# Convolution taps, level sums and gate copies moved between engines in a four-part transformer kernel on one Trainium2 core

## The chip, the cores and the metric

The kernel runs on one core of a Trainium2 chip. The metric is the device time of one execution in microseconds (us). A core has five engines with queues of their own: TensorE (PE; its weight loads are listed apart as PEld), VectorE (DVE), ScalarE (ACT), GpSimd (POOL) and SyncE (SP), which here issues the loads of weights. Each engine takes its instructions in the order of the program and waits on semaphores for the others. PSUM, where TensorE writes, is used as eight banks.

## The reference, cut to what matters

There are 256 tokens of width 1024. They pass an even layer (a convolution branch and gated linear attention), a PEER layer (128 chosen experts of 16384 a token), an odd layer (attention with forget gates), a second PEER layer, and then a block of sliding-window attention with spatial gating (mix2) and an MLP with a three-tap convolution. The parts that the change touches:

```python
def conformer_conv(val, gate, conv_w, conv_b, ln_g, ln_b):      # even layer, 512 channels, 31 taps
    u = val * jax.nn.sigmoid(gate)
    y = lax.conv_general_dilated(u, w, window_strides=(1,), padding=[(CONV_WIDTH - 1, 0)], ...)
    y = y + conv_b.astype(y.dtype)
    return jax.nn.silu(layer_norm(y, ln_g, ln_b))
...
def step(state, inp):                                           # even layer, gated linear attention
    b = jnp.cumsum(gi, axis=2)
    o_inter = jnp.einsum('bhtk,bhkv->bhtv', qi * jnp.exp(b), state)
    decay = jnp.exp(jnp.where(causal[:, :, None], diff, -jnp.inf))
    attn = jnp.einsum('bhtk,bhsk,bhtsk->bhts', qi, ki, decay)
    o = o_inter + jnp.einsum('bhts,bhsv->bhtv', attn, vi)
...
def block(args):                                                # PEER
    ht, et, gt = args
    act = jax.nn.gelu(jnp.einsum('td,ted->te', ht, u[et]), approximate=False)
    return jnp.einsum('te,ted->td', gt * act, v[et])
...
q = rms_norm(q.reshape(B, S, FOX_HEADS, FOX_HD), q_g)           # odd layer
k = rms_norm(k.reshape(B, S, FOX_HEADS, FOX_HD), k_g)
...
x = x + conv_gated_mlp(rmsnorm(x, ffn_norm[l]), w_up[l], conv_w[l], conv_b[l], w_down[l])
```

## The kernel before

Activations lie with the width on the 128 partitions and the tokens along them. Every dense product takes its float32 operands in two parts, a rounded one (`_hi`) and the rest (`_lo`), so that one block of weights costs three products: hi x hi, lo x hi, hi x lo. Weights pass a **Stream**: SyncE loads a block of 512 KB into `w_raw`, ScalarE rounds it to `w_hi` (L337), VectorE subtracts for `w_lo` (L353). All dense products are issued at line L452.

What runs beside a projection is written as generators. `tick` (L900) steps the list **flow** once and gives **bg**, the background, an allowance of ns; so the place of small steps between the large products follows from their yields. `banks(pj, pa, pl, po)` gives the PSUM banks that projections and auxiliary products go round in.

The even layer (0 to about 175 us) projects v (`va`, four steps, `natural`), the channels of the convolution (`aval`, `agate`), k and q (`kq`) and r. `gated` makes a channel block `ub` = val x sigmoid(gate) (the tanh of `sg` on ScalarE, L941, and the product L942). Of its 31 taps 23 go to VectorE as multiply-adds `yc` in the background (`conv`, L769), and the first 8 (`CONV_PE`) to TensorE: GpSimd scales eight diagonals `dg` (`taps`, L656), `conv_pe` multiplies them with ub into a bank `pe`, ScalarE copies it to `yp` (L783). `decays` makes the decays of the attention. `inner`, once for each of 8 pairs of head and token half, makes seven levels of scores `pm`, VectorE masks them to `sm` (L822, L823), and seven products add them up in `oT`, after which products with the state follow. A chain of `inner` begins in each tick. `head_norm` (products `o_ps`, `ob`) and `layer_norm` (`mu_b`, `var_ps`, `rs_b`) give the rows `yf` of the output projection, whose blocks (`rows`) are added as their rows become ready.

A PEER layer runs 64 gate cycles (369 to 604 us, and 1351 to 1586 us), each of 4 tokens: ScalarE makes one-hot rows `oa` (L1168, four; L1174), VectorE their partners `ob`, TensorE the gates `g` of the cycle into PSUM and 24 products `pu`, the experts' activations; ScalarE and VectorE write gelu(pu) into X (L1271 on ScalarE, L1274 and L1275 for the later part). `put` (below) takes the gates of the cycle out of PSUM: where X has activations already, they are multiplied (L1190), elsewhere copied (L1192, VectorE). The copied part shrinks from 308 to about 56 columns in the 64 cycles.

```python
                    for lo, hi, x in spans(c, NCH):
                        nc.vector.tensor_copy(x[:, :, t0:t0 + GT], gt[:, lo:hi])
```

In the odd layer `qk_out` squares each q or k block (`qk_sq`, L1527) and after each second k block adds `quad` to flow, which begins `rms_heads`: eight small products `qn_ps`, the root, and their spread `qn_rb`. `c_ps` are the sums of the forget gates; `pt` are transposes of the attention. `mix2` uses banks 4 to 7 for projections and 0 to 3 for the rest. In the MLP `normed` makes the normalised input of the later products: GpSimd multiplies by `rb` (L1749) and by the gain (L1750), ScalarE rounds (L1752), GpSimd subtracts to `hn_lo` (L1754), for 8 blocks.

Of the kernel before, what the change touches and what calls it, by code (L numbers as in the profile page):

```python
# [20 lines left out]
P = 128  # L21
# [20 lines left out]
EV_ROWS = (4, 5, 6, 7, 0, 1, 2, 3)  # L42
CONV_PE = 8
U_SLACK = 1300
# [334 lines left out]
def body(ctx: ExitStack, tc: tile.TileContext, a, out, phases=(0, 6)):  # L379
# [6 lines left out]
    class Banks:  # L386
# [5 lines left out]
        def set(self, banks):  # L392
            self.banks, self.i = banks, 0
# [244 lines left out]
    def even():  # L638
        banks((0, 1), (2, 3))
        with even_pool as es:  # L640
# [7 lines left out]
            tri64, = masks(sp, 3, 4)  # L648
            dgs = deque()

            def taps():
                c = len(dgs) + pe_done
                if c < 4:
                    dg = tp.tile([P, CONV_PE, P], F32, name="dg", tag="dg")
                    for j in range(CONV_PE):
                        nc.gpsimd.tensor_scalar(dg[:, j], ident, col("convw", c * CONVW + j), None, op0=OP.mult)  # L656
                    dgs.append(dg)

            f2 = lambda t: t.rearrange("p a b -> p (a b)")
# [5 lines left out]
            def parts(k0, n):  # L665
                for k in range(k0, k0 + n):
                    if k in split_k:
                        i = split_k.index(k)
                        split_to(y[0][:, i], y[1][:, i], yf[:, k])
                    ready.add(k)  # L670

# [17 lines left out]
            def decays():  # L689
# [7 lines left out]
                proj_small(h, gws, ps[:16, :S], 16)  # L697
                while norm["steps"] is not None:
                    yield
# [64 lines left out]
            def conv(c):  # L764
                nc.vector.tensor_scalar(yc[:, c], ub[:, c, CONV_PE:CONV_PE + S], col("convw", c * CONVW + CONV_PE),
                                        col("convb", c), op0=OP.mult, op1=OP.add)
                yield 300
                for j in range(CONV_PE + 1, CONVW):
                    nc.vector.scalar_tensor_tensor(yc[:, c], ub[:, c, j:j + S], col("convw", c * CONVW + j),  # L769
                                                   yc[:, c], op0=OP.mult, op1=OP.add)  # L770
                    yield 400

            pe_done = 0

            def conv_pe(c):

                nonlocal pe_done
                pe = acc(3, "pe")
                dg = dgs.popleft()
                for j in range(CONV_PE):  # L780
                    mm(pe[:, :S], dg[:, j], ub[:, c, j:j + S], j == 0, j == CONV_PE - 1)
                yield
                nc.scalar.activation(yp[:, c], pe[:, :S], AF.Copy)  # L783
                pe_done += 1
                taps()

# [24 lines left out]
            def inner(hd, tb):  # L811

                p, e = divmod(hd, 2)
                pr = slice(e * 64, (e + 1) * 64)
                ts = slice(tb * P, (tb + 1) * P)
                pm = [psum.tile([P, 512], F32, tag=f"bank{i}", name="pm") for i in pm_banks]
                for l, (za, zb) in enumerate(zl):
                    mm(pm[l // 4][:, (l % 4) * P:(l % 4 + 1) * P], za[pr, p, ts], zb[pr, p, ts],
                       l % 4 == 0, True)
                yield  # L820
                sm = tp.tile([P, 7, P], F32, name="sm", tag="sm", bufs=2)
                nc.vector.tensor_mul(f2(sm[:, :4]), pm[0], f2(lmask[:, :4]))  # L822
                nc.vector.tensor_mul(f2(sm[:, 4:]), pm[1][:, :3 * P], f2(lmask[:, 4:]))  # L823
                yield
                if not oT:
                    oT.extend(psum.tile([P, 512], F32, tag=f"bank{i}", name="oT") for i in range(2))
                for l in range(7):
                    mm(oT[p][:, e * S + tb * P:e * S + (tb + 1) * P], vn[:, tb, hd * P:(hd + 1) * P], sm[:, l],
                       p not in started, l == 6)
                    started.add(p)  # L830
                for c in (2 * tb, 2 * tb + 1):
                    if c > 0:
                        mm(oT[p][:, e * S + c * 64:e * S + (c + 1) * 64], stt[:, p, c - 1],
                           qe[:, e, p, c * 64:(c + 1) * 64], False, True)
                yield
# [53 lines left out]

            ready = set()  # L890
            chains = deque(inner(2 * p + e, tb) for p in range(2) for tb in range(2) for e in range(2))
# [8 lines left out]
            def tick(n, slack):  # L900
                for _ in range(n):
                    if "levels" in done:
                        if "states" not in done:
                            done.add("states")
                            flow.add(states())
                        elif chains:
                            flow.add(chain(chains.popleft()))
                    flow.step()
                    bg.run(slack)
# [5 lines left out]
            for j in range(4):  # L915
                natural(va, j)
                if j == 1:
                    flow.add(decays())
                if j >= 2:
                    taps()  # L920
                flow.step()
# [7 lines left out]
            def branch(c):  # L929
# [7 lines left out]
                def gated():  # L937
                    sg = tp.tile([P, S], F32, name="sg", tag="t256")
                    nc.vector.tensor_mul(sg, pg[:, :S], rb)

                    nc.scalar.activation(sg, sg, AF.Tanh, scale=0.5)  # L941
                    nc.vector.scalar_tensor_tensor(ub[:, c, 30:], sg, 1.0, va_sb, op0=OP.add, op1=OP.mult)  # L942
                    bg.add(conv(c))
                    flow.add(conv_pe(c))

# [6 lines left out]
            for t, scale in ((kT, 1.0), (qT, 0.125)):  # L952
                for p in range(2):
# [3 lines left out]
                    tick(1, E_SLACK)  # L957
            banks((4, 5), (3,))
            flush()
# [13 lines left out]
            while len(chains) > E_LATE:  # L973
                tick(1, E_SLACK2)
            pm_banks[1] = 3
            rows = Rows(y, [split_k.index(k) if k in split_k else k for k in EV_ROWS], yf)
            while rows.n < 6:
# [12 lines left out]
    def peer(l):  # L990
        banks((0, 1, 4, 5), (2, 3))
        with ExitStack() as es:
# [161 lines left out]
            def gates():  # L1154
# [31 lines left out]
                def put(t0, g):  # L1186
# [4 lines left out]
                    for lo, hi, x in spans(c, NCH):  # L1191
                        nc.vector.tensor_copy(x[:, :, t0:t0 + GT], gt[:, lo:hi])  # L1192
                    done["t"] = t0 + GT
# [232 lines left out]
    def odd():  # L1426
        banks((4, 5, 6, 7), (0, 1, 2, 3))
        with ExitStack() as es:
# [86 lines left out]

            def quad(b):
                yield from rms_heads(lambda b: qk[:, b], qz, lambda b: sq[:, slot(b)], [b, 8 + b, b + 1, 9 + b], [gq, col("odk"), gq, col("odk")], tp, bd64)
                if b == 6:
# [43 lines left out]
    def mix2():  # L1562
        banks((4, 5, 6, 7), (0, 1, 2, 3))
        with ExitStack() as es:
# [168 lines left out]
    def mlp():  # L1733
        banks((0, 1, 4, 5, 6, 7), (2, 3))
        with ExitStack() as es:
# [9 lines left out]
            def normed():  # L1745

                for k in range(KD + 2):
                    if k < KD:
                        nc.gpsimd.tensor_tensor(room[:, k], xT[:, k], rb, op=OP.mult)  # L1749
                        nc.gpsimd.tensor_scalar(room[:, k], room[:, k], col("ffn2", k), None, op0=OP.mult)  # L1750
                    if 0 <= k - 1 < KD:
# [96 lines left out]
```

## Time and profile before

| what | value |
|---|---|
| median of three runs | 2348.55 us (2344.61 to 2349.74) |
| the profiled execution, its own time | 2352.38 us |
| its span | 2350.6 us |
| TensorE busy | 2315.8 us, 99% of the span |
| VectorE busy | 1723.3 us, 73% |
| ScalarE busy | 1357.8 us, 58% |
| GpSimd busy | 93.6 us, 4% |
| DMA | 386.82 MB, 165 GB/s in the mean |

The profile counts an engine as busy while an instruction of it runs. Matmuls overlap each other, so a share of 99% says that TensorE has seldom nothing under way, and not that it runs at its best; the granted clock (a share of full speed) is read beside it. A row of a wait names who waited, on which line, and for which engine's instruction. The profiled execution is one of its own and 3.8 us above the median.

### The profile page before, as it was taken

The numbers are of one execution on the slowest core, as the hardware profiler recorded it, in microseconds if no ns is written. First come the engines' busy times: TensorE is split into PE (matmuls) and PEld (weight loads), VectorE is DVE, ScalarE is ACT, GpSimd is POOL, SyncE is SP. The second block draws the span as 40 slices with busy tenths as digits, with TensorE's granted clock in tenths as the row PEclk, the third lists the DMA queues.
The fourth block names the chain that finished last, engine by engine and source line by source line (L and its number), as shares of the span: only waits on it lengthen the run. The fifth ranks groups of instructions, "written<-read, shape, count | busy, mean of one in ns | idle before, by whom it ended". The sixth has DMA issues, their size and how long they took to land. (4 is left out here: it accounts for less than half of the span.)

```text
span 2350.6 us, 48812 instructions
## 1 busy us (share of the span) xinstructions
PE 2315.8 (99%) x19664; PEld 2268.3 (97%) x19664; DVE 1723.3 (73%) x3656; ACT 1357.8 (58%) x2480; POOL 93.6 (4%) x107
## 2 busy tenths in 40 slices
PE   8999999999999999999999999999999999999999
PEld 7889999999999999998899999999999999999999
DVE  6668999999755555566699899996555555667983
ACT  6226448888544444455564588884444445555762
POOL 4100000000000000010000000000000000002300
PEclk9899999999999999999999999999999999999999
DMA  6114654444555666553256544446556565645553
GB/s 214 54 63 163 193 185 156 149 145 140 174 185 185 206 186 184 178 193 117 89 165 190 186 145 147 144 142 188 185 185 206 185 185 161 210 137 177 181 182 123
DMA packets 106626, 386.82 MB, mean 165 GB/s; under 512 B 11959, under 2 KB 13272, under 8 KB 106016
## 3 DMA queue, kind: packets, MB, share of 16 engines
q1 hardware_dynamic: 104976, 377.99, 50.7%
q0 software_dynamic: 1136, 5.32, 0.7%
q8 instruction: 154, 2.52, 0.4%
q14 instruction: 72, 0.59, 0.1%
q10 hardware_dynamic: 288, 0.40, 0.1%
HBM read 383.40 MB, written 1.05 MB: 164 GB/s over the span
## 5 line engine op out<-in xcount | busy, mean ns | idle before, releaser
L353 DVE TENSOR_TENSOR w_lo<-w_raw,w_hi 128x1024 fp32r<-128x1024 f32 x710 | 866.4, 1224 | 383.9 <-ACT w_hi L337 382.3
L337 ACT ACTIVATE w_hi<-w_raw 128x1024 fp32r<-128x1024 f32 x710 | 745.6, 1054 | 432.6 <-PE pv L452 348.0
L452 PE MATMUL pu<-h_hi,w_hi 128*128 128x256 f32 x2048 | 586.9, 287 | 0.0
L452 PE MATMUL pu<-h_lo,w_hi 128*128 128x256 f32 x2048 | 575.2, 281 | 0.0
L452 PE MATMUL pu<-h_hi,w_lo 128*128 128x256 f32 x2048 | 574.5, 281 | 0.0
L452 PE MATMUL pv<-h_hi,w_hi 128*128 128x256 f32 x1888 | 530.4, 281 | 0.0
L452 PE MATMUL pv<-h_lo,w_hi 128*128 128x256 f32 x1888 | 530.4, 281 | 0.0
L452 PE MATMUL pv<-h_hi,w_lo 128*128 128x256 f32 x1888 | 530.4, 281 | 0.0
L452 PEld LDWEIGHTS pu<-h_lo,w_hi 128*128 128x128 f32 x2048 | 386.4, 189 | 0.0
L452 PEld LDWEIGHTS pu<-h_hi,w_lo 128*128 128x128 f32 x2048 | 385.8, 188 | 0.0
L452 PEld LDWEIGHTS pu<-h_hi,w_hi 128*128 128x128 f32 x2048 | 385.5, 188 | 0.0
L452 PEld LDWEIGHTS pv<-h_hi,w_lo 128*128 128x128 f32 x1888 | 355.8, 188 | 0.0
L452 PEld LDWEIGHTS pv<-h_lo,w_hi 128*128 128x128 f32 x1888 | 355.8, 188 | 0.0
L452 PEld LDWEIGHTS pv<-h_hi,w_hi 128*128 128x128 f32 x1888 | 355.8, 188 | 0.0
L1271 ACT ACTIVATE X<-pu 128x256 f32<-128x256 f32 (+31 forms) x228 | 74.1, 325 | 197.2 <-PE pu L452 197.1
L1168 ACT ACTIVATE oa<-cb,routed 128x128 bf16<-128x128 f32 x512 | 162.9, 398 | 0.0
L1173 DVE TENSOR_TENSOR ob<-ob,g 128x512 bf16<-128x512 bf16 x256 | 108.0, 422 | 4.4
L452 PEld LDWEIGHTS <-oa 128*128 128x128 bf16 x1536 | 90.2, 96 | 12.9 <-issue 5.3
L452 PE MATMUL g<-ob,oa 128*128 128x128 bf16 x1024 | 102.1, 219 | 0.0
L452 PE MATMUL g<-oa 128*128 128x128 bf16 x512 | 94.7, 219 | 0.3
L461 DVE TENSOR_TENSOR h_lo<-X,h_hi 128x512 fp32r<-128x512 f32 (+1 forms) x134 | 86.4, 653 | 2.1 <-ACT h_hi L460 1.9
L1174 ACT ACTIVATE oa<-oa 128x512 bf16<-128x512 bf16 x128 | 80.8, 631 | 4.1
(450 smaller groups left out, 4122.3 us busy)
## 6 DMA issues: line engine op xcount, KB each, us to landing
w_raw<-in_s_u SPq DMA_DIRECT2D x256, 512.0 KB, 3.6
w_raw<-in_s_v SPq DMA_DIRECT2D x256, 512.0 KB, 3.6
w_raw<-in_s_mix SPq DMA_DIRECT2D x46, 512.0 KB, 3.9
w_raw<-in_s_up SPq DMA_DIRECT2D x44, 512.0 KB, 4.3
w_raw<-in_s_wq SPq DMA_DIRECT2D x32, 512.0 KB, 3.7
w_raw<-in_s_odd SPq DMA_DIRECT2D x32, 512.0 KB, 4.0
w_raw<-in_s_even SPq DMA_DIRECT2D x28, 512.0 KB, 3.9
w_raw<-in_s_down SPq DMA_DIRECT2D x22, 512.0 KB, 4.2
```

The source lines that it names most:

```text
L337: self.nc.scalar.activation(hi, raw, AF.Copy)
L353: self.nc.vector.tensor_sub(lo, raw, hi.bitcast(F32))
L452: nc.tensor.matmul(o, l, r, start=start, stop=stop, skip_group_check=True)
L461: nc.vector.tensor_sub(lo, src, hi.bitcast(F32))
L1168: nc.scalar.activation(o[0][:, i * P:(i + 1) * P], iota, AF.Abs, bias=ne1T[:, t0 + i:t0 + i + 1])
L1173: nc.vector.tensor_tensor(two[part], two[2], pairs(g3[:, part, t0:t0 + GT]), op=OP.mult)
L1174: nc.scalar.activation(o[0], o[0], AF.Relu, bias=1.0, scale=-1.0)
L1271: nc.scalar.activation(X(c)[:, td:], ps[:, td:S], AF.Gelu)
```

## The change

Seven things change; the layout of the stages and the dense products stay.

1. Even layer: the 8 taps of each channel block leave TensorE. ScalarE writes the block scaled by one tap to `yp` (the first) or `tap` (the other seven, four buffers), and GpSimd adds them up in `yp`: 32 copies, 28 additions. The diagonals and their products go.
2. Even layer: in `inner` GpSimd adds the seven masked levels of `sm` to one (an addition of 384 columns and three of 128), and one product in `oT` takes the place of seven. A yield more stands ahead of it, `sm` has three buffers.
3. Even layer: `decays` begins after the first of four steps of v and waits for the sums of the norm; bank 7 is lent to the auxiliary products for a while; a block of rows is ready only from the next tick on (`late`).
4. PEER: the copies of `put` go from VectorE to ScalarE.
5. Odd: `quad` yields once before it begins.
6. mix2: projections go round in six banks, the rest in two.
7. MLP: the gain is applied by ScalarE from the input, ahead of `rb`, which GpSimd multiplies in after it.

```diff
-                if j == 1:
+                if j == 0:
                     flow.add(decays())
-                if j >= 2:
-                    taps()
...
-                while norm["steps"] is not None:
+                while norm["steps"] is not None or norm["n"] < KD:
                     yield
...
-                    ready.add(k)
+                    late.add(k)
...
+            def conv_pool(c):
+
+                for j in range(CONV_POOL):
+                    t = tp.tile([P, S], F32, name="tap", tag="tap", bufs=4) if j else yp[:, c]
+                    nc.scalar.activation(t, ub[:, c, j:j + S], AF.Copy, scale=col("convw", c * CONVW + j))
+                    if j:
+                        nc.gpsimd.tensor_tensor(yp[:, c], yp[:, c], t, op=OP.add)
+                    if j % 2:
+                        yield
...
-                sm = tp.tile([P, 7, P], F32, name="sm", tag="sm", bufs=2)
+                sm = tp.tile([P, 7, P], F32, name="sm", tag="sm", bufs=3)
...
+                add = lambda o, a_, b_: nc.gpsimd.tensor_tensor(o, a_, b_, op=OP.add)
+                add(f2(sm[:, 0:3]), f2(sm[:, 0:3]), f2(sm[:, 3:6]))
+                add(sm[:, 2], sm[:, 2], sm[:, 6])
+                add(sm[:, 0], sm[:, 0], sm[:, 1])
+                add(sm[:, 0], sm[:, 0], sm[:, 2])
+                yield
                 yield
...
-                for l in range(7):
-                    mm(oT[p][:, e * S + tb * P:e * S + (tb + 1) * P], vn[:, tb, hd * P:(hd + 1) * P], sm[:, l],
-                       p not in started, l == 6)
-                    started.add(p)
+                mm(oT[p][:, e * S + tb * P:e * S + (tb + 1) * P], vn[:, tb, hd * P:(hd + 1) * P], sm[:, 0],
+                   p not in started, True)
+                started.add(p)
...
+                    ready.update(late)
                     flow.step()
                     bg.run(slack)
...
-            banks((4, 5), (3,))
+            banks((4, 5), (3, 7))
             flush()
             done.add("qk")
...
             pm_banks[1] = 3
+            banks((4, 5), (3,))
...
-                        nc.vector.tensor_copy(x[:, :, t0:t0 + GT], gt[:, lo:hi])
+                        nc.scalar.activation(x[:, :, t0:t0 + GT], gt[:, lo:hi], AF.Copy)
...
             def quad(b):
+                yield
                 yield from rms_heads(...)
...
     def mix2():
-        banks((4, 5, 6, 7), (0, 1, 2, 3))
+        banks((4, 5, 6, 7, 0, 1), (2, 3))
...
-                        nc.gpsimd.tensor_tensor(room[:, k], xT[:, k], rb, op=OP.mult)
-                        nc.gpsimd.tensor_scalar(room[:, k], room[:, k], col("ffn2", k), None, op0=OP.mult)
+                        nc.scalar.activation(room[:, k], xT[:, k], AF.Copy, scale=col("ffn2", k))
+                        nc.gpsimd.tensor_tensor(room[:, k], room[:, k], rb, op=OP.mult)
```

How the order moves, at three places. On GpSimd in the even layer, between the sums of the norm at its start (`sqacc`) and those at its end, as a piece of the difference:

```order
-L656 TENSOR_SCALAR dg<-cb,cols 128x128 x32
+L769 TENSOR_TENSOR yp<-yp,tap 128x256 x26
+L811 TENSOR_TENSOR sm<-sm 128x384
+L811 TENSOR_TENSOR sm<-sm 128x128 x3
+L769 TENSOR_TENSOR yp<-yp,tap 128x256 x2
+L811 TENSOR_TENSOR sm<-sm 128x384
```

The diagonals go; 26 of the 28 additions of taps stand ahead of the first head's sums, and the eight heads' sums follow each other, four additions each.

On ScalarE in the gates, one cycle before:

```order
L1168 ACTIVATE oa<-cb,routed 128x128 x4
L1174 ACTIVATE oa<-oa 128x512
L337 ACTIVATE w_hi<-w_raw 128x1024
L1271 ACTIVATE X_1484<-pu 128x216
L1274 ACTIVATE gl<-pu 128x40
```

and a cycle of the changed kernel (its lines are 8 lower):

```order
L1160 ACTIVATE oa<-cb,routed 128x128 x4
L1166 ACTIVATE oa<-oa 128x512
L1184 ACTIVATE X_1480<-g 128x72x4
L337 ACTIVATE w_hi<-w_raw 128x1024
L1263 ACTIVATE X_1480<-pu 128x232
L1266 ACTIVATE gl<-pu 128x24
```

The copy of the gates (72 columns of four tokens here) stands between the one-hot rows and the rounding of the weights.

On TensorE in the odd layer, around the sums of the forget gates, before:

```order
L452 MATMUL c_ps<-lf,masks 128x16
L452 MATMUL c_ps<-lf,cb 128x16
L452 MATMUL c_ps<-lf,masks 128x16
L452 MATMUL c_ps<-masks,lf 16x128
L452 MATMUL c_ps<-cb,lf 16x128
L452 MATMUL c_ps<-masks,lf 16x128
L452 MATMUL qn_ps<-masks,qk_sq 128x2 x8
L452 MATMUL qk_ps<-h_hi,w_hi 128x256
```

and now:

```order
L452 MATMUL c_ps<-cb,lf 16x128
L452 MATMUL c_ps<-masks,lf 16x128
L452 MATMUL qk_ps<-h_hi,w_hi 128x256
L452 MATMUL qk_ps<-h_lo,w_hi 128x256
L452 MATMUL qk_ps<-h_hi,w_lo 128x256
```

The small products qn_ps no longer follow c_ps at once; a block of 24 products of q or k stands between them.

## Rows read from the trace of the kernel before

**Rows 1.** busy us by stretch: start:end, length, PE, PEld, DVE, ACT, POOL, clock

```profile
50.00:95.00 45.00, 41.08 (x282) 38.13 (x282) 36.36 (x73) 15.52 (x29) 8.28 (x8) 0.92 0.29 93
95.00:152.00 57.00, 52.69 (x356) 49.36 (x355) 39.31 (x84) 6.73 (x12) 0.00 (x0) 0.88 0.09 30
```

**Rows 2.** TensorE's waits over the span: who for what, total us, times, longest us

```profile
PE pe L452 <- DVE ub L942: 3.4, 2, 2.5
PE pt L1392 <- ACT pts L1394: 1.8, 4, 0.6
PE va L452 <- DVE gt L1599: 1.6, 1, 1.6
PE qn_ps L452 <- ACT qk_sq L1527: 1.6, 1, 1.6
PE up L452 <- DVE w_lo L353: 1.4, 1, 1.4
PE up L452 <- POOL hn_lo L1754: 1.3, 2, 1.0
```

**Rows 3.** groups by line and shape, even layer: busy us, mean ns, idle before

```profile
L452 PE MATMUL pe<-ub,dg 128*128 128x256 f32 x64 | 16.3, 412 | 3.4 <-DVE ub L942 3.4
L452 PE MATMUL oT<-sm,vn 128*128 128x128 f32 x112 | 15.8, 298 | 0.0
```

**Rows 4.** VectorE's waits in 28 to 152 us: total us, times, longest us

```profile
DVE sr L967 <- PE r L452: 17.2, 4, 8.9
DVE ub L942 <- ACT sg L941: 4.6, 4, 3.1
```

**Rows 5.** in order of time, even layer's end: start, length, instruction, idle before it

```profile
173.25 0.48 DVE L486 SCALAR_TENSOR_TENSOR h_lo<-xT,cols,h_hi 128x256 fp32r<-128x256 f32 x1
...
174.25 1.02 DVE L486 SCALAR_TENSOR_TENSOR h_lo<-xT,cols,h_hi 128x256 fp32r<-128x256 f32 x1
174.26 0.73 POOL L494 TENSOR_TENSOR sqacc<-sqacc,z 128x256 f32<-128x256 f32 x1 [97.53 <-ACT z L492]
```

**Rows 6.** VectorE's groups by shape, 2164 to 2194 us, GpSimd busy beside

```profile
L353 DVE TENSOR_TENSOR w_lo<-w_raw,w_hi 128x1024 fp32r<-128x1024 f32 x8 | 11.5, 1440 | 0.0
L1771 DVE SCALAR_TENSOR_TENSOR z<-zi,cols,z 128x255 f32<-128x255 f32 x9 | 6.6, 731 | 0.2 <-ACT z L1768 0.2
L1780 DVE TENSOR_TENSOR sg<-sg,z 128x256 f32<-128x256 f32 x3 | 2.9, 964 | 0.0
```

**Rows 7.** VectorE's groups by shape, 2200 to 2280 us, GpSimd idle

```profile
L353 DVE TENSOR_TENSOR w_lo<-w_raw,w_hi 128x1024 fp32r<-128x1024 f32 x31 | 37.7, 1216 | 0.0
L1771 DVE SCALAR_TENSOR_TENSOR z<-up,cols,z 128x255 f32<-128x255 f32 x30 | 14.4, 480 | 5.3 <-ACT z L1768 4.8
L1780 DVE TENSOR_TENSOR sg<-sg,z 128x256 f32<-128x256 f32 x16 | 6.7, 419 | 0.0
```

**Rows 8.** TensorE in order of time, before the even layer's last normalisations

```profile
143.92 3.67 PE L452 MATMUL rows<-yf,w_raw 128*128 128x256 f32 x16
```

**Rows 9.** TensorE in order of time: first products of gate cycles

```profile
369.36 0.28 PE L452 MATMUL pu<-h_hi,w_hi 128*128 128x256 f32 x1
...
394.57 0.36 PE L452 MATMUL pu<-h_hi,w_hi 128*128 128x256 f32 x1
...
398.18 0.37 PE L452 MATMUL pu<-h_hi,w_hi 128*128 128x256 f32 x1
...
603.95 0.37 PE L452 MATMUL pu<-h_hi,w_hi 128*128 128x256 f32 x1
```

**Rows 10.** gates: the copy (min/median/max ns), ScalarE's read of PSUM, a stretch

```profile
L1192 DVE COPY X<-g x128: 206/338/469, 378.9 to 1590.5; 128x308 f32<-128x308 f32 x2, 128x304 f32<-128x304 f32 x2, 128x300 f32<-128x300 f32 x2, 128x296 f32<-128x296 f32 x2
...
L1271 ACT ACTIVATE X<-pu 128x256 f32<-128x256 f32 x3 | 1.1, 377 | 2.0 <-PE pu L452 2.0
...
400.00:450.00 50.00, 50.00 (x501) 49.27 (x500) 49.08 (x125) 43.99 (x112) 0.00 (x0) 1.00 0.47 147
```

**Rows 11.** busy time by stretch, odd layer: PE, PEld, DVE, ACT, POOL, clock, DMA

```profile
1048.00:1050.00 2.00, 2.00 (x11) 2.00 (x11) 0.82 (x1) 2.00 (x4) 0.00 (x0) 0.50 0.21 18
```

More of the change, by code (lines that the diff above doesn't have):

```diff
@@ L42 @@
 EV_ROWS = (4, 5, 6, 7, 0, 1, 2, 3)
-CONV_PE = 8
+CONV_POOL = 8
 U_SLACK = 1300
@@ L648, in even @@
             tri64, = masks(sp, 3, 4)
[L649 to L657, printed above, removed]
             f2 = lambda t: t.rearrange("p a b -> p (a b)")
@@ L764, in conv @@
             def conv(c):
-                nc.vector.tensor_scalar(yc[:, c], ub[:, c, CONV_PE:CONV_PE + S], col("convw", c * CONVW + CONV_PE),
+                nc.vector.tensor_scalar(yc[:, c], ub[:, c, CONV_POOL:CONV_POOL + S], col("convw", c * CONVW + CONV_POOL),
                                         col("convb", c), op0=OP.mult, op1=OP.add)
                 yield 300
-                for j in range(CONV_PE + 1, CONVW):
+                for j in range(CONV_POOL + 1, CONVW):
                     nc.vector.scalar_tensor_tensor(yc[:, c], ub[:, c, j:j + S], col("convw", c * CONVW + j),
@@ L771, in conv @@
                     yield 400
[L773 to L784, printed above, removed]
-                taps()
+            def conv_pool(c):
[6 more added lines that the diff above has]
+                        yield
             def states():
@@ L888, in layer_norm @@
                 yield
-            ready = set()
+            ready, late = set(), set()
             chains = deque(inner(2 * p + e, tb) for p in range(2) for tb in range(2) for e in range(2))
@@ L916, in even @@
                 natural(va, j)
-                if j == 1:
+                if j == 0:
                     flow.add(decays())
-                if j >= 2:
-                    taps()
                 flow.step()
@@ L943, in gated @@
                     bg.add(conv(c))
-                    flow.add(conv_pe(c))
+                    flow.add(conv_pool(c))
                 proj_t(h, pg[:, :S], then=gated)
```

## The prediction

> **What bounds the kernel now.** I read the busy shares first: TensorE is busy in 99% of the span, so a gain can only come from places where TensorE waits, where it runs at its lower clock, or where its work is taken away while nothing else is just as long. The table by stretch then shows where that is. In two stretches of the even layer TensorE is short of full: in 50 to 95 us it is busy 41.08 of 45 us and in 95 to 152 us 52.69 of 57, and at granted clocks of 0.92 and 0.88 [rows 1]. VectorE is busy 36.36 and 39.31 us there, so it is idle for 8.64 + 17.69 = 26.3 us. The list of TensorE's waits names six other places that the change touches, none above 3.4 us [rows 2]. So nearly all that can be won is in the even layer (which ends near 175 us), in the two runs of 64 gate cycles, and in single waits. 0.2% of the time, 4.7 us, is about what a measurement of this kernel can tell from no change.
>
> **Even layer: taps and level products.** TensorE loses its 64 tap records (16.3 us and a wait of 3.4) and six of seven level products per head (15.8 us of records for all of them, 13.5 of it) [rows 3]. These 30 us aren't the gain: much of VectorE's work stands on the same path, 23 convolution taps for each of four channels, that the change leaves where they are. What TensorE gives up is worth what VectorE waits for it. VectorE's waits in 28 to 152 us are mainly four for `r`, 17.2 us in all and 8.9 the longest, and four for `sg`, 4.6 in all [rows 4]. With the tap products gone from ahead of the r blocks and one product for seven between them I expect the waits for r to shrink to about 4 us (the last two blocks, which still stand behind a head's products), and three waits for sg to stay (4.6 - 3.1 = 1.5). So 26.3 - 5.4 = 21 us of VectorE's idle time can go.
>
> Against it stands GpSimd. It had 32 scalings of a diagonal there; now it has 28 additions of 128x256 and, for eight heads, 768 columns of additions each, as much as 3 x 8 = 24 more of that size: 52 additions that read two operands from SBUF. The trace shows what such an addition does to VectorE beside it: at 174.25 us an `h_lo` takes 1.02 us while GpSimd adds for 0.73, and the one before, beside nothing, 0.48 [rows 5], so 0.54 us for one addition. The MLP's start shows it in bulk: there GpSimd does 8 multiplications by rb and 8 subtractions for hn_lo, 16 instructions with two operands, and in these 30 us eight w_lo take 1440 ns, nine z 731 and three sg 964 [rows 6], where the same shapes take 1216, 480 and 419 later [rows 7]. That is 1.8 + 2.3 + 1.6 = 5.7 us, 0.36 for each of the 16. I take 0.36, since VectorE's mix of PSUM readers and two-operand work there is nearest to that of the even layer; the ends are 0 and 0.73. So 52 x 0.36 = 18.7 us, of which about 4 fall into waits that stay anyway: 14.7 us come back on VectorE.
>
> At the end of the layer the order costs something. Today a block of the output projection's products (`rows`, 3.67 us) stands between the steps of the last normalisations [rows 8]; in the new order these steps stand in a row and the blocks come after them. I put it at one such block, 3.7 us (ends 0 and 7.4, two blocks). ScalarE's 32 scaled copies and GpSimd's latency of four additions per head (the extra yield puts the next head's products between) I cost at nothing: ScalarE is busy for only 15.52 of 45 and 6.73 of 57 us [rows 1]. If that cover fails, GpSimd sets the pace, at 3 x 0.73 = 2.2 us a head, which is no more than the two-head distance hides. Starting the decays earlier frees no wait of the size of these; I leave it out. **Even: 26.3 - 5.4 - 14.7 - 3.7 = 2.5 us gained**, between -16.8 (0.73 per addition) and +17 (0).
>
> The Trainium skill has a rule that speaks against this part: "SBUF — State Buffer", section "SBUF: two separate sides", says that VectorE and GpSimd share one pair of ports as an exclusive lock, and that the one that comes second is blocked for the other's whole instruction. The row at 174.25 us agrees that there is a block (0.54 of the addition's 0.73), not that it lasts for all of it on average; by the rule the even layer would lose, and this is rival B below.
>
> **Gates.** A PEER layer's 64 gate cycles run from 369.36 to 603.95 us, 234.6 us or 3.665 each; a cycle in which TensorE runs without a gap is 394.57 to 398.18, 3.61 [rows 9]. The difference, 64 x 0.055 = 3.5 us a layer, comes from cycles late in the run, where VectorE is full (49.08 of 50 us busy already at 400 to 450). The copies that leave VectorE took 206 to 469 ns, median 338 [rows 10]; with 0.34 us less in a cycle of 3.6, VectorE stops holding it. ScalarE takes them: it is busy 43.99 of 50 us, so 3.18 of 3.61 us a cycle, and reads 256 columns of PSUM in 377 ns [rows 10]; the mean copy has 182 columns, so I take 0.33 us, which gives 3.51, below 3.61. The first copies, of 308 columns, bring it to about 3.60, level with TensorE. **Gates: 2 x 3.5 = 7 us gained**, ends -2 (the early cycles each 0.03 us late) and 8.
>
> **Odd layer.** The extra yield puts a block of q/k products ahead of each `qn_ps`. The wait for qk_sq (1.6 us) [rows 2] has 24 products over it then, so it goes. After it TensorE runs at its lower clock: in 1048 to 1050 us it is busy throughout at 0.50 of full (1.2 of 2.4 GHz) [rows 11]; with its neighbours that costs 1.7 us. A second such spell, after c_ps and qn_ps one behind the other, costs as much; the two are separated now. Against this, one rows block less stands over the last transposes, which wait 1.8 us in four pieces today [rows 2]: -1. **Odd: 1.6 + 1.7 + 1.7 - 1 = 4 us gained**, ends 0 and 5.
>
> **Mix2 and MLP.** With six banks for the projections, `va` no longer waits for the reader of the bank (1.6 us) [rows 2]: **1.6**, ends 0 and 1.6. In the MLP GpSimd loses a third of its 24 instructions, and ScalarE's scaling needs no rb, so it can run ahead; TensorE's waits for hn_lo (1.3) and for a w_lo slowed beside it (1.4) go [rows 2]: **2.7**, ends 0 and 2.7. What comes next there is only w_lo's supply, which is ahead in the stretch behind.
>
> **Sum.** 2.5 + 7 + 4 + 1.6 + 2.7 = 17.8 us. The profiled execution took 2352.4 us, 3.8 above the median of the runs; 2352.4 - 17.8 = 2334.6, and on the scale of the median 2331 us.
>
> **Rivals.** A: the additions cost VectorE nothing, because GpSimd takes gaps that VectorE leaves (its waits, its reads of PSUM). For it: 26.3 us of gaps are there now; against: the MLP's start, where gaps did not help [rows 6, 7]. Even is then +17, the sum 32.5, the time 2316. B: each addition holds VectorE for its full 0.73 us: 52 x 0.73 - 4 = 34 us, even -16.8, the sum -1.5, so 2350. For it speaks that one h_lo lost 0.54, against it the mean of 0.36. C, the slower end: ScalarE becomes the bound of the gate cycle. The copy reads four separate pieces of a PSUM tile, and no ScalarE row shows that form. If it costs twice the plain read of its width, 0.64 us, the cycle is 3.18 + 0.64 = 3.82 instead of 3.665: 128 x 0.155 = 20 us lost instead of 7 gained, the sum -9, the time 2358. It decides from a copy of 0.57 us (a cycle of 3.75, 11 us lost, which eats the other 10.8). Against it: PSUM reads of odd widths on ScalarE follow their column count in this trace. D: the gates gain nothing, as another VectorE instruction holds the late cycles: 2338.
>
> **How the numbers follow.** The forecast 0.53, A 0.18, B 0.13, C 0.05, D 0.11. Of B, half ends within 4.7 us and the rest is split; C is slower. Faster by over 0.2% (below 2343.9): 0.53 + 0.18 + 0.11 + 0.03 = 0.85; within 0.2%: 0.09; slower 0.06. The range leaves out C, the worse half of B and the far end of A: 2313 to 2347.
>
> **What would show it.** In the changed kernel: the waits of VectorE for r below 5 us (else TensorE wasn't relieved); yc above 484 ns and the additions above 0.73 where the two meet, with an excess near 19 us in all (0: A; 38: B); 64 gate cycles in 231 us and X copies on ScalarE near 0.33 us (C: 0.6, and TensorE waiting for ScalarE); no wait of qn_ps, va or up in TensorE's list, and no stretch at 0.50 near 1048 us. The forecast is wrong if the even layer, up to its last rows product, changes by more than 10 us either way, or if the gate cycle isn't 3.61.

## The result and the profile after

The changed kernel takes 2507.88 us in the median (2507.0 to 2508.27, four runs), the kernel before 2348.82. The ratio is 1.068, with a 95% interval of 1.0662 to 1.0699: slower by 159 us, where 18 us of gain were forecast and 2313 to 2347 us was the range. The profiled execution has a span of 2506.2 us, 155.6 more than that of before.

The page's busy shares and its row of TensorE in 40 slices show at once that it isn't spread over the span:

```profile
PE 2317.0 (92%) x19504; PEld 2266.5 (90%) x19504; DVE 1715.8 (68%) x3528; ACT 1397.8 (56%) x2644; POOL 98.3 (4%) x127
PE   7789998777799999999899987777999999999999
```

TensorE is busy for as long as before, 2317 us, but in 92% of the span. Apart from the first two slices, which are in the even layer, the sevens stand in two stretches, which are the two runs of gate cycles. Cut by the first product of each stage (pv by its first product with h_hi; 5.8 us of products with oa and ob ahead of it count to the row above), the two profiled executions compare as follows:

| stage (us) | before | after | difference |
|---|---|---|---|
| even layer, to the first query projection | 181.5 | 195.7 | +14.2 |
| first PEER's query projection | 47.7 | 47.2 | -0.5 |
| first PEER, 64 gate cycles and the products pu | 423.2 | 493.6 | +70.5 |
| its products pv | 358.2 | 358.2 | 0.0 |
| odd layer | 152.2 | 156.0 | +3.8 |
| second PEER to its pv | 471.7 | 541.2 | +69.5 |
| its pv | 358.2 | 358.2 | 0.0 |
| mix2 | 159.2 | 157.8 | -1.4 |
| MLP, up to its last projection | 131.8 | 131.3 | -0.4 |
| the rest | 67.1 | 67.0 | -0.1 |

The sum of the exact differences is 155.6. The gates carry 140 of it, and the even and the odd layer went the wrong way too.

TensorE's waits over the whole span (who for what, total us, times, longest) answer to [rows 2]:

```profile
PE g L452 <- ACT X L1184: 131.9, 122, 1.2
PE pm L452 <- DVE sm L808: 11.0, 7, 3.4
...
PE r L452 <- DVE va_sb L923: 5.9, 1, 5.9
PE rows L452 <- ACT y_hi L460: 5.9, 7, 0.9
PE aval L452 <- DVE va_sb L923: 5.7, 2, 3.9
...
PE up L452 <- DVE w_lo L353: 2.6, 2, 1.6
```

The first one did not exist before: the gates' products wait 122 times, 1.1 us each, until ScalarE's copy has read their PSUM tile. One cycle in order of time, of ScalarE, VectorE and the first gate product, shows why the copy is late:

```profile
482.41 0.36 ACT L1184 ACTIVATE X<-g 128x232 f32<-128x232 f32 x1 [1.30 <-DVE X L1182]
482.67 1.05 ACT L337 ACTIVATE w_hi<-w_raw 128x1024 fp32r<-128x1024 f32 x1
482.83 0.22 PE L452 MATMUL g<-oa 128*128 128x128 bf16 x1 [1.02 <-ACT X L1184]
...
483.75 1.23 DVE L353 TENSOR_TENSOR w_lo<-w_raw,w_hi 128x1024 fp32r<-128x1024 f32 x1 [1.38 <-ACT w_hi L337]
...
484.90 0.24 DVE L1267 TENSOR_TENSOR X<-X,gl 128x80 f32<-128x80 f32 x1
485.05 0.42 DVE L1162 TENSOR_TENSOR ob<-iota,e2b 128x512 bf16<-128x512 bf16 x1
...
485.50 0.42 DVE L1165 TENSOR_TENSOR oa<-ob,g 128x512 bf16<-128x512 bf16 x1
485.85 0.88 DVE L1165 TENSOR_TENSOR ob<-ob,g 128x512 bf16<-128x512 bf16 x2
486.64 0.51 DVE L1182 TENSOR_TENSOR X<-g,X 128x176 f32<-128x176 f32 x2
487.19 0.36 ACT L1184 ACTIVATE X<-g 128x228 f32<-128x228 f32 x1 [1.31 <-DVE X L1182]
```

It is a ring through two engines. The copy waits for VectorE's multiplication of the other part of the same gates (487.19 after 486.64). Behind the copy on ScalarE stands the rounding of the next weights, w_hi. Behind that, on VectorE, waits w_lo (1.38 us), and behind w_lo, in VectorE's order, the one-hot work and the next multiplication. Once round is 487.19 - 482.41 = 4.78 us, against 3.61 for a cycle of TensorE without gaps [rows 9]. Neither engine is full (in 450 to 600 us VectorE is busy for 70% of the time and ScalarE for 71%): between them they hand one another the turn, and TensorE waits for the pair.

### The profile page after: what moved, and what is told of

It reads as the page before. It is cut to its first block, busy times and chain, and to the rows that moved or that the text cites. A ratio compares the mean times of both kernels' runs of the same rounds, so it can differ in the third digit from the quotient of the medians.

```text
span 2506.2 us, 48441 instructions
## 1 busy us (share of the span) xinstructions
PE 2317.0 (92%) x19504; PEld 2266.5 (90%) x19504; DVE 1715.8 (68%) x3528; ACT 1397.8 (56%) x2644; POOL 98.3 (4%) x127
## 3 DMA queue, kind: packets, MB, share of 16 engines
q1 hardware_dynamic: 104976, 377.99, 48.9%
## 5 line engine op out<-in xcount | busy, mean ns | idle before, releaser
L452 PEld LDWEIGHTS <-oa 128*128 128x128 bf16 x1536 | 98.1, 96 | 145.9 <-issue 140.1
L1184 ACT ACTIVATE X<-g 128x308 f32<-128x308 f32 (+42 forms) x128 | 41.2, 322 | 180.0 <-DVE X L1182 180.0
```

Source lines behind the costliest of these rows:

```text
L452: nc.tensor.matmul(o, l, r, start=start, stop=stop, skip_group_check=True)
L1184: nc.scalar.activation(x[:, :, t0:t0 + GT], gt[:, lo:hi], AF.Copy)
```

## Experiments

### The gates

The first four runs ask whether the ring is the cause, whether it needs the other parts, and what the parts are worth without it. In e1_copy_first the two loops of `put` are exchanged in the changed kernel:

```diff
-                    for lo, hi, x in spans(0, c):
-                        nc.vector.tensor_mul(x[:, :, t0:t0 + GT], gt[:, lo:hi], x[:, :, t0:t0 + GT])
                     for lo, hi, x in spans(c, NCH):
                         nc.scalar.activation(x[:, :, t0:t0 + GT], gt[:, lo:hi], AF.Copy)
+                    for lo, hi, x in spans(0, c):
+                        nc.vector.tensor_mul(x[:, :, t0:t0 + GT], gt[:, lo:hi], x[:, :, t0:t0 + GT])
```

> The changed kernel, with the two loops of put exchanged: the copy on ScalarE is issued ahead of VectorE's multiplication, so that it no longer waits for it (both read the bank of g). Nothing else moves. Theory ring (the copy waits for the multiplication, the rounding of the weights stands behind the copy on ScalarE, w_lo behind the rounding, and the multiplication behind w_lo on VectorE): the ring of 4.77 us a cycle is cut, cycles return to 3.60 to 3.67 us, 128 x 1.1 = 141 us go, the time is 2362 to 2370. Rival work (ScalarE has too much to do with the copies on it): ScalarE does the same work in the same order, the time stays at 2490 to 2510.

It took 2361.31 us (2360.28 to 2363.49), ratio 1.0057 (1.004 to 1.0074), a little under the 2362 to 2370 of the theory: 147 us go by the order of two loops. The stretch from the first pu to the first pv is 420.7 us in both layers, against 493.6 and, before, 423.2. Its cycle:

```profile
480.97 0.33 ACT L1182 ACTIVATE X<-g 128x208 f32<-128x208 f32 x1
481.19 1.05 ACT L337 ACTIVATE w_hi<-w_raw 128x1024 fp32r<-128x1024 f32 x1
481.57 0.53 DVE L1184 TENSOR_TENSOR X<-g,X 128x176 f32<-128x176 f32 x2
```

The copy waits for nothing and w_hi starts ahead of the multiplication. The ring is gone, and the copies at the middle of the run stand 3.6 us apart. ScalarE's work is the same, so the rival of too much work falls: its copies take 310 ns in the mean in 400 to 600 us.

In e2_gates_only the kernel before has the copy of `put` on ScalarE, behind the multiplication, and nothing else:

```diff
-                        nc.vector.tensor_copy(x[:, :, t0:t0 + GT], gt[:, lo:hi])
+                        nc.scalar.activation(x[:, :, t0:t0 + GT], gt[:, lo:hi], AF.Copy)
```

> The kernel before, with the copy of put on ScalarE and nothing else of the change. Theory ring: the whole loss of the gates stands alone, 2 x 70 us: 2485 to 2492. Rival (the loss needs another part of the change, such as the even layer's different state of the weight stream): clearly less than 2470.

2487.2 us, ratio 1.059 (1.0569 to 1.0611), and 493.6 us from pu to pv: the gates' loss stands alone.

e3_before_copy_first is the kernel before with both of these edits, so with the copy on ScalarE and ahead of the multiplication.

> The kernel before, with the copy on ScalarE and issued ahead of the multiplication. Theory ring: the cycle falls to about 3.61 us, as VectorE is relieved of 0.34 us in it: 2 x 3.5 = 7 us gained, 2341 to 2345. Rival work: ScalarE is at 3.18 + 0.32 = 3.50 us of a cycle of 3.61, too near; it holds the early cycles with the widest copies, and the time is 2350 to 2370.

2344.53 us against 2347.95 beside it, ratio 0.9987 (0.9977 to 0.9996). From pu to pv it is 420.8 us, 2.4 less a layer. So the gain that the change was after is there, 5 us in the traces and 3.4 in the medians, where 7 were worked out. ScalarE doesn't hold up the early cycles, which take 3.60 us each; the late ones still take 3.64 to 3.71.

A fourth run asks if the wait itself costs, or what stands behind it. In g4_copy_later the changed kernel's copy still follows the multiplication and still waits for it, but is issued after the next w_hi:

```diff
-                    for lo, hi, x in spans(c, NCH):
-                        nc.scalar.activation(x[:, :, t0:t0 + GT], gt[:, lo:hi], AF.Copy)
+                    def copy():
+                        for lo, hi, x in spans(c, NCH):
+                            nc.scalar.activation(x[:, :, t0:t0 + GT], gt[:, lo:hi], AF.Copy)
+                    held.append(copy)
...
                 proj_t(h, ps[:, :S])
+                copies()
                 td = done["t"]
...
```

> The changed kernel (2508) with the copy still behind VectorE's multiplication and still waiting for it, but issued after the rounding of the next weights (w_hi) on ScalarE instead of ahead of it. Theory ring: the wait itself is harmless, what counts is that w_hi stood behind it; without w_hi in the ring the cycle returns to 3.6 to 3.75 us: 2361 to 2380. Rival (any wait of the copy for the multiplication costs, since the bank of g comes free later): the cycle stays over 4.3 us and the time over 2450.

2368.4 us, and 422.7 us from pu to pv. Its cycle shows w_hi ahead of the multiplication and the copy right behind it:

```profile
483.44 1.05 ACT L337 ACTIVATE w_hi<-w_raw 128x1024 fp32r<-128x1024 f32 x1
483.79 0.53 DVE L1188 TENSOR_TENSOR X<-g,X 128x176 f32<-128x176 f32 x2
484.39 0.32 ACT L1191 ACTIVATE X<-g 128x208 f32<-128x208 f32 x1
```

The copy is still tied to the multiplication, but ScalarE stands idle for it in only one of the first layer's 64 cycles, where in the changed kernel it stood idle in all 64, for 1.4 us in the mean. So the tie by itself costs little (2 us a layer more than in e1_copy_first); what cost 70 us a layer is that the weights stood behind it. The tie can be read in the traces' records: each of the 128 copies waits for a semaphore that VectorE's multiplications raise in the changed kernel, in e2_gates_only and in g4_copy_later, and none of them does in e1_copy_first and e3_before_copy_first, where the copy goes first. The two write different columns of X; what they share is the PSUM tile g that both read. The Trainium skill's page "PSUM — Partial Sum Buffer", section "PSUM bank collisions raise a hardware error", says that two engines may not touch the same part of a bank at once, that reads count, and that the scheduler adds a dependency between any two such instructions of different engines. No run here lets the two overlap, which wasn't tried, and none shows that the shared tile is the reason for the tie; that the tie follows the program's order is what the records show.

### The even layer

e4_no_even is the changed kernel with the even layer of before.

> The changed kernel, with the even layer as in the kernel before (taps and level products on TensorE, decays as before). Theory: the parts are independent, the even layer's 14 us go: 2491 to 2496, and the first product of the first PEER layer's query projection starts at 181 to 182 us. Rival: the even layer's delay is taken up again by waits of the stages behind it: 2503 to 2508.

2491.6 us (2488.05 to 2495.16), so 16 us go, and the first query projection starts at 175.3 us. That this isn't 181.5 shows something that one trace can't: the same code of the even layer ends at 181.5, 173.6, 178.7, 175.3, 179.9 and 177.1 us in the six profiled executions that have it, with mean granted clocks of 0.88 to 0.97 in 95 to 152 us. The changed layer ends at 195.7, 194.7 and 195.8. So the profiled execution of before is the slowest of six, whose mean is 177.7, and the layer's loss is nearer to 18 us in the mean of the traces than to the 14.2 of the table.

In the changed kernel's trace, the stretches that answer to [rows 1], and then VectorE's taps and GpSimd's groups in 28 to 160 us:

```profile
50.00:95.00 45.00, 33.14 (x249) 31.56 (x247) 43.22 (x74) 23.16 (x48) 16.30 (x20) 0.85 0.30 94
95.00:152.00 57.00, 43.71 (x210) 40.45 (x211) 46.94 (x81) 7.48 (x13) 26.01 (x38) 0.64 0.00 1
```

```profile
L759 DVE SCALAR_TENSOR_TENSOR yc<-ub,cols,yc 128x256 f32<-128x256 f32 x88 | 54.5, 650 | 1.2
L734 DVE TENSOR_TENSOR z<-z,kT 128x256 f32<-128x256 f32 x6 | 4.1, 687 | 0.0
L735 DVE TENSOR_TENSOR z<-z,qT 128x256 f32<-128x256 f32 x6 | 4.1, 682 | 0.0
...
L769 POOL TENSOR_TENSOR yp<-yp,tap 128x256 f32<-128x256 f32 x28 | 24.2, 871 | 57.5 <-ACT tap L767 56.5
L811 POOL TENSOR_TENSOR sm<-sm 128x128 f32<-128x128 f32 x24 | 12.8, 546 | 1.3
L811 POOL TENSOR_TENSOR sm<-sm 128x384 f32<-128x384 f32 x8 | 9.0, 1131 | 18.4 <-DVE sm L809 18.4
```

The 88 taps take 54.5 us; before they took 39.7, 484 ns each. Counted one by one in this trace, the 35 taps that run while GpSimd does nothing take 481 ns in the mean, and the 53 that overlap an addition 761. With z (8.2 us, before 2.9 + 2.5) and qe that is 14.8 + 2.8 + 0.2 = 17.8 us more of VectorE's time. TensorE, which is now short of work and waits for VectorE (seven waits for sm, 11 us), runs at 0.64 of its full clock in the second stretch: of its two levels, mostly the one of 1.2 GHz.

Four runs take e1_copy_first, which is the changed kernel without the ring, and undo pieces of the even layer. f3_one_operand lets GpSimd copy the second operand instead of adding:

```diff
-                        nc.gpsimd.tensor_tensor(yp[:, c], yp[:, c], t, op=OP.add)
+                        nc.gpsimd.tensor_copy(yp[:, c], t)
...
-                add = lambda o, a_, b_: nc.gpsimd.tensor_tensor(o, a_, b_, op=OP.add)
+                add = lambda o, a_, b_: nc.gpsimd.tensor_copy(o, b_)
```

> e1_copy_first (2361) with each of GpSimd's additions in the even layer replaced by a copy of its second operand, same shapes, same count, same waits; so the eight taps and the seven levels aren't summed. Theory port, in the form that it takes two operands on GpSimd: yc returns to about 485 ns, 15 to 18 us of VectorE's time go, 2346 to 2352. Rival any work (anything that GpSimd does beside VectorE costs the same): yc stays at 600 ns or more and the time at 2357 to 2363.

2349.6 us, 11.7 below e1_copy_first. In its trace, VectorE's taps and GpSimd's copies:

```profile
L759 DVE SCALAR_TENSOR_TENSOR yc<-ub,cols,yc 128x256 f32<-128x256 f32 x88 | 43.0, 520 | 1.2
```

```profile
L769 POOL COPY yp<-tap 128x256 f32<-128x256 f32 x28 | 15.2, 547 | 57.2 <-ACT tap L767 56.2
```

Most of the excess goes, 11.4 of 14.7 us on the taps, but not all: 520 is not 484. Copies are shorter too (547 ns against 871), but that isn't enough to explain it: 46.0 us of additions cost the taps 14.7, and 29.5 us of copies 3.3. So the form "two operands" carries most of it, and some is left for one operand. f4_no_additions drops the additions:

```diff
-                    if j:
-                        nc.gpsimd.tensor_tensor(yp[:, c], yp[:, c], t, op=OP.add)
...
-                add(f2(sm[:, 0:3]), f2(sm[:, 0:3]), f2(sm[:, 3:6]))
-                add(sm[:, 2], sm[:, 2], sm[:, 6])
-                add(sm[:, 0], sm[:, 0], sm[:, 1])
-                add(sm[:, 0], sm[:, 0], sm[:, 2])
```

> e1_copy_first (2361) without GpSimd's additions in the even layer at all: only the first of the eight taps and the first of the seven levels are used. Theory port: yc at 484 ns, z at 415 to 475, and since no one waits for GpSimd either, 2344 to 2350. Rival order (even without any cost on VectorE the layer ends late, since the last normalisations stand in a row and TensorE idles into its lower clock): 2354 to 2360.

2345.68 us, 15.6 below e1_copy_first. The taps are back at their own length, and yet VectorE still waits for r:

```profile
L759 DVE SCALAR_TENSOR_TENSOR yc<-ub,cols,yc 128x256 f32<-128x256 f32 x88 | 39.4, 482 | 1.2
```

```profile
DVE sr L951 <- PE r L452: 11.1, 3, 6.4
DVE ub L926 <- ACT sg L925: 4.5, 4, 3.1
```

This run separates the terms, as far as one trace of it can. The first mu_b is where the convolution's norm begins; it comes here, and then in the kernel before and in e2_gates_only, which has the same even layer, at:

```profile
L452 PE MATMUL mu_b<-yc,cb x8: 379/379/379, 138.4 to 139.9; 128*128 128x256 f32 x8
```

```profile
L452 PE MATMUL mu_b<-yc,cb x8: 379/379/483, 150.7 to 152.3; 128*128 128x256 f32 x8
```

```profile
L452 PE MATMUL mu_b<-yc,cb x8: 380/631/792, 141.3 to 144.4; 128*128 128x256 f32 x8
```

In the changed kernel it comes at 156.6, so the additions cost about 18 us. What the work taken from TensorE is worth depends on the execution of the old layer beside it: 12.3 us against 150.7, but the other five have mu_b at 141.3 to 147.5, so 3 to 12 us, and 7 in the mean of six. And from mu_b to the first query projection it takes 39.0 us here, as in the changed kernel (39.1), against 30.8 before and 32.3 to 32.5 in the other five: about 7 us are lost at the layer's end whatever GpSimd does. In the mean -7 + 18 + 7 = 18 us is the layer's loss; against the profiled execution of before alone it is -12.3 + 18.2 + 8.3 = 14.2.

f1_taps_back and f2_sums_back bring one half back to TensorE each:

```diff
...
-                    flow.add(conv_pool(c))
+                    flow.add(conv_pe(c))
```

> e1_copy_first (2361) with the eight taps of a channel on TensorE again, by diagonals that GpSimd scales; the level sums stay on GpSimd. Theory port (GpSimd's additions of two operands slow VectorE's instructions beside them, 17.9 us in the even layer by the changed kernel's rows): 28 of 52 units of addition go, so about 10 us of VectorE's time: 2350 to 2355, and yc falls from 650 to about 560 ns. Rival order (the loss comes from the order of the layer's end and from TensorE's idle time): TensorE has more to do, so 2358 to 2366.

2361.65 us, no change, as the rival had it. The taps' yc fell to 587 ns, 5.5 us in all (54.4 - 48.9), and the layer ended at 191.8 us in the trace, 3.0 earlier than in e1_copy_first, but in the runs nothing of it is left: in the trace the stages behind the layer take 4.4 us longer than in that of e1_copy_first, and why stays open. The clock in 95 to 152 us is 0.64 as with the taps away, so it doesn't hang on them:

```profile
95.00:152.00 57.00, 46.13 (x220) 42.33 (x219) 43.81 (x74) 4.52 (x7) 21.12 (x32) 0.64 0.03 9
```

f2_sums_back takes out the four additions with their yield, gives `sm` two buffers again and brings the seven products back:

```diff
...
-                mm(oT[p][:, e * S + tb * P:e * S + (tb + 1) * P], vn[:, tb, hd * P:(hd + 1) * P], sm[:, 0],
-                   p not in started, True)
+                for l in range(7):
+                    mm(oT[p][:, e * S + tb * P:e * S + (tb + 1) * P], vn[:, tb, hd * P:(hd + 1) * P], sm[:, l],
+                       p not in started, l == 6)
...
```

> e1_copy_first (2361) with seven level products per head again instead of GpSimd's sums (and without the yield that came with them); the taps stay on ScalarE and GpSimd. Theory port: the sums' share, 24 of 52 units, about 8 us of VectorE's time, goes, and TensorE has 13.5 us of products more, mostly in time in which it waited: 2352 to 2358. Rival order: the products keep TensorE busy and its clock up, so that more goes than VectorE's share: below 2350.

2351.81 us, 9.5 below e1_copy_first, just under the theory's range and not as far as the rival's; yc 559 ns, the clock 0.93 in 95 to 152 us:

```profile
95.00:152.00 57.00, 49.83 (x353) 46.56 (x353) 43.66 (x88) 8.46 (x16) 5.18 (x7) 0.93 0.10 33
```

VectorE's taps take 8.0 us less (54.4 - 46.4). In the trace the layer ends 10.6 us earlier, 5.5 of them ahead of mu_b and 5.1 behind it (34.0 us from mu_b to the first query projection instead of 39.1). With seven products TensorE has 13.5 us more to do, and still the layer is shorter: the sums were the worse half of the change.

g3_no_late takes up the layer's end. There TensorE's steps stand in a row, at 0.50 of full clock in 164 to 172 us (changed kernel):

```profile
156.62 1.89 PE L452 MATMUL mu_b<-yc,cb 128*128 128x256 f32 x8
160.11 1.02 PE L452 MATMUL o_ps<-cb,osq 128*128 128x1 f32 x8 [1.60 <-ACT csq L862]
161.49 2.53 PE L452 MATMUL var_ps<-cb,csq 128*128 128x1 f32 x16 [0.35 <-ACT ors L838]
164.37 1.12 PE L469 MATMUL ob<-cb,ors 128*128 128x128 f32 x4 [0.35 <-ACT cst L868]
166.26 0.69 PE L469 MATMUL rs_b<-cb,cst 128*128 128x128 f32 x2 [0.78 <-DVE sr L845]
167.50 0.58 PE L452 MATMUL rows<-y_hi,w_hi 128*128 128x256 f32 x1 [0.55 <-ACT y_hi L460]
```

```diff
-                    late.add(k)
+                    ready.add(k)
```

> e1_copy_first (2361) with a block of rows ready at once again (ready instead of late); all else of the even layer as changed. The order of TensorE then has a block of 24 products of rows between ob and rs_b at the end of the layer. Theory cover: from mu_b to the first query projection the changed kernel takes 39.1 us, the kernel before 30.9; with the block as cover 1 to 3 us come back: 2358 to 2361, and 36 to 38 us from mu_b. Rival: the tail's length is set by the lower clock after the wait alone: 39 us stay.

2364.12 us, and 39.3 us from mu_b: the block now stands ahead of rs_b, but it waits 2.0 us for its own y_hi, right behind ob, and runs at the lower clock. That theory fell. The traces show two things more of these 39 us. TensorE's mean clock in them is 0.87, by which about 5 us are lost (an estimate, 0.13 x 39); in the old layer's six executions the stretch loses 0 to 2 us in this way. And the 12 products of the last head's norm (o_ps, ob) stand behind mu_b, where in the kernel before and in f2_sums_back they stand ahead of it. In f2_sums_back 5 of the 7 us are gone, with that order, seven products and one yield less per head; which of these does it stays open.

### The odd layer, and the best version

g2_odd_yield is the kernel before with the extra yield alone:

```diff
             def quad(b):
+                yield
                 yield from rms_heads(...)
```

> The kernel before with the extra yield in every quad, as in the change, and nothing else. Theory: the yield moves the pair chains one block later, so each of the six rows blocks stands too near to the po that it needs and waits 0.89 us, and a block's cover is lost besides; the gain of 3 to 5 us at qn_ps is given back and more: +3.8 us, 2350 to 2353. Rival: the odd layer's loss in the changed kernel came with the later stream position or another part; here the yield gains 4 us, 2343 to 2345.

2351.27 us against 2347.33, ratio 1.0018 (1.0009 to 1.0028), with the odd layer at 156.0 us as in the changed kernel. The waits of the changed kernel's odd layer show where it goes:

```profile
PE rows L452 <- ACT y_hi L460: 5.3, 6, 0.9
```

In the first half the yield does what was forecast: from the first q/k product to the first v product g2_odd_yield takes 58.8 us instead of 64.1, and no stretch is at 0.50 [rows 11]. But the attention pairs that the last quad starts come one block later too. Before, the first rows block follows the second `po`; now it follows the first one, and each of six blocks waits 0.89 us for rows that were made just ahead of it, and then takes 3.4 us instead of 3.0. The second half takes 97.2 us instead of 88.1; the waits are 5.4 of these 9.1 us, the longer blocks some 2.4, and the rest isn't accounted for.

So in g1_best only the first three quads yield; it has also e3's edits, and mix2's and the MLP's edits of the change:

```diff
             def quad(b):
+                if b < 6:
+                    yield
                 yield from rms_heads(...)
```

> The kernel before with what gained or should gain: the copy of put on ScalarE ahead of the multiplication (e3_before_copy_first, 2344.5), mix2's banks, the MLP's gain on ScalarE, and the extra yield in quad for the first three quads only, so that the pair chains of the odd layer start where they did. Theory: mix2 -1.5, MLP -0.4 (as in the changed kernel's trace), odd -3 to -5 (no wait of qn_ps, no spell at 0.50, and no wait of rows for y_hi): 2337 to 2341. Rival (the rows' waits in the odd layer come from any later quad, not from the last one): odd +3 to +4, 2345 to 2349.

2336.51 us (2334.08 to 2340.37) against 2347.33, ratio 0.9955 (0.9942 to 0.9969), better than both kernels by more than the interval, and just under the 2337 to 2341 of the theory. Its odd layer takes 146.9 us, 5.3 less than before, and up to the sums of the next layer's norm its waits there are down to one name:

```profile
PE pt L1392 <- ACT pts L1394: 0.9, 2, 0.6
```

## Why the prediction was wrong

**Gates, the step that failed.** The prediction priced the moved copy by ScalarE's busy time: 3.18 + 0.33 = 3.51 us, below 3.61. This sum is right; e1_copy_first and e3_before_copy_first run it. The step that failed is the wait, which the prediction put at nothing: it never asked what the copy waits for on its new engine. On VectorE it stood behind the multiplication by order alone; on ScalarE it has to wait for it, and w_hi, which was free to run ahead, is queued behind. The cycle became the ring of 4.78 us instead of 3.61. Rival C named the right place and sign, ScalarE as the one to be waited for, but by a slow copy of 0.64 us (the copies took 0.32), at 20 us. The loss was 140 us, by a mechanism that was on no list of the prediction.

**Even layer.** Of its three terms, the price of the additions was right where it looked boldest: 18.7 us of VectorE's time were worked out from 0.36 for an addition, and 17.8 came. By the Trainium skill's rule in "SBUF — State Buffer", section "SBUF: two separate sides", a block for the whole instruction would give at most 46 us (an estimate: GpSimd's whole busy time, if VectorE was always there to be blocked); the measured 17.8 is well below that. The rows behind the 0.36 compare z from `zi` with z from `up` [rows 6, 7]; with GpSimd idle both take 481 ns in that trace, so the reading holds, though it charges nothing to GpSimd's eight products with the gain, which ran in the same stretch. Four of the 18.7 were to fall into waits that stay; in the traces the additions cost about 18 us, so hardly any did (15.6 us in the medians). The credit was too high: 21 us were to come from VectorE's waits, and 3 to 12 came, 7 in the mean. The waits for r were to shrink to 4 us; they are 7.8 in the changed kernel's trace and 11.1 with all the additions away. The 17.2 us [rows 4] that they were to shrink from belonged to that one execution; in the five others of the same code they are 9.2 to 14.0. And the end of the layer cost about 7 us instead of 3.7, as TensorE's steps wait for each other and run at the lower clock besides.

**Odd layer.** The gains, 5.0 us in the prediction's terms, came: 5.3 us. The loss of "one rows block less" was put at 1 us; it is 9.1, since not one cover is lost but each of six blocks comes too near to its source. (Of the 1.8 us of waits for pts [rows 2], which the prediction gives to this layer, half stand in mix2.) As g1_best shows, the loss wasn't needed.

**mix2 and MLP.** mix2 gained 1.4 of 1.6. In the MLP the waits for hn_lo went, as forecast, and the waits for w_lo grew from 1.4 to 2.6: 0.4 us gained instead of 2.7, which is no more than executions with the old MLP differ by (125.2 to 125.9 us in four, from up to dn; 125.3 in the changed kernel). The prediction had named w_lo's supply as next and taken it to be ahead.

**The chances.** 0.06 for slower was too small for a change that puts new instructions ahead of the weights in a queue that feeds everything else. By the prediction's own parts it should have been about 0.08 (C's 0.05 and a quarter of B's 0.13). And rival C's price was bounded by the copy's own length, which bounds nothing where a wait comes with it.

## What to carry to other kernels

An instruction that is moved to another engine brings its dependencies with it: list what it waits for there, and what of that engine's work is queued behind it, before adding up busy times. If that queue feeds the engine that it waits for, it is a ring, and its length, not anyone's busy share, is the cycle; exchanging two loops can cut it. An engine that gives work away beside a full one gains only what the full one waits for, and an order that gives one wait more room should be followed to the end of the stage, where it may take the room from another.

## What the runs showed of the hardware that was not expected

Additions on GpSimd that read two operands lengthen VectorE's two-operand instructions beside them: 484 to 650 ns in the mean of 88 taps with 46 us of additions in the stretch, 761 for the 53 that overlap one, and 520 in the mean where GpSimd only copies (29.5 us). Taking work from TensorE can lower its clock: 0.88 to 0.97 in 95 to 152 us with seven products a head, 0.64 to 0.74 with one (0.74 without any additions on GpSimd), and 0.93 when the seven came back with the taps still away.
